# The first stage of an encoder trunk: c loaded into every partition, x loaded by tokens and turned on TensorE, the scale columns computed one contraction tile at a time

## The chip, the cores and the metric

The kernel runs on one core of a Trainium2 chip. A core has TensorE (PE, matrix products; its weight loads are listed apart as PEld), VectorE (DVE), ScalarE (ACT), GpSimd (POOL) and the sync engine (SP), which here issues nearly all DMA transfers. The metric is the device time of one execution in microseconds (us), lower is better. A difference of 0.2% (about 2.1 us here) is what a measurement can tell from no change.

## The reference, cut to what matters

Two layers, each FFN, mixer, FFN. The change touches only the start of the first FFN of layer 0: the conditioning vector `c`, the RMSNorm of `x`, and the first six of 22 column groups of the product with `ffn1_w13`.

```python
c_act = jax.nn.silu(c)                                   # c: (1, 1024)
cond = (c_act @ ada_w[l] + ada_b[l])[:, None, :]         # ada_w[l]: (1024, 9 * 1024)
sh1, sc1, g1, sh2, sc2, g2, sh3, sc3, g3 = jnp.split(cond, 9, axis=-1)
...
y = xf * lax.rsqrt(jnp.mean(xf * xf, axis=-1, keepdims=True) + RMS_EPS)   # rmsnorm(x, norm_g)
h = rmsnorm(x, norm_g[l, 0]) * (1 + sc1) + sh1           # x: (256, 1024)
a, g = jnp.split(h @ ffn1_w13[l], 2, axis=-1)            # (1024, 2 * 2816)
x = x + 0.5 * g1 * ((silu(g) * a) @ ffn1_w2[l])
```

## The kernel before, in words

Activations lie with features on partitions: `xT` is 128 partitions x 8 feature tiles x 256 tokens. Every large product is made of three float32r products: weight and activation are each split into a rounded part and a rest (`whi`, `wlo`; `hh`, `hl`), and `mm3` (lines 236 to 240) issues high by high (L238), high by low (L239) and low by high (L240). ACT makes `whi` (L220), DVE makes `wlo` (L221), `raw` being the loaded weight.

The first stage, `first_in` (L450 to L529), is recorded so that each engine keeps the order in which the code stands (`in_order`), while the engines run free of one another. It loops over the eight feature tiles k of the contraction; a k has 36 products of 128x128 weights by 256 tokens, into six PSUM banks that stay open over the whole stage. Ahead of a product of tile k stand: the shift column, a DVE sum of a 128x1024 piece of `ada_w` with `cact`, silu of c in all partitions (`cond_sum`, L279); the scale column; the normalised tile `xr` (L423), its parts `hh` (ACT, L427) and `hl` (DVE, L428); and the two halves of the weight, split.

The scale columns come from TensorE instead. `ada_rows` (L297 to L302) takes a piece of `ada_w` and the column form of silu(c), `ck`, in eight one-row products that go to partitions 0, 32, 64 and 96 of one bank; ACT copies the bank (`arow`, L463); `ada_cols` (L304) turns the rows into columns by a product with ones; DVE adds the bias and scales (L312, L295). Before, one piece serves two k: four pieces of 128x2048, the first ahead of the loop, the others at the ends of k = 0, 2 and 4, with their `ada_cols` in the middle of k = 1, 3 and 5.

Ahead of the loop, `c` is loaded as one row, spread over the partitions by a product with ones (`spread_c`, L180), and run through silu; `xT` is loaded as it lies in HBM (the host has turned it); ACT squares its eight tiles (L354), DVE adds them (L359), TensorE sums over partitions (L367), POOL takes the power -1/2 (L389, listed as L105), TensorE spreads the result (L394), ACT copies it out as `R`. In the gaps TensorE gets warm-up products of a zero tile (`warm_up`, L192): 11, 0, 2 and 6 of them.

All loads go through SP, in program order. At most eight transfers are outstanding: a ninth waits for the first to land. Buffers: six of 128x2048 for weights and scale pieces, three for shift pieces.

Of the kernel before, what the change touches and what calls it, by code (L numbers as in the profile page):

```python
# [15 lines left out]
P = 128  # L16
# [39 lines left out]
NW = 11, 0, 2, 6  # L56
# [13 lines left out]
def trunk_kernel(  # L70
# [92 lines left out]
    def load_consts(r0):  # L163
        sp.dma_start(out=ck, in_=ck_in)
        sp.dma_start(out=xT[:, :4], in_=xT_in[:, :4])
        sp.dma_start(out=xT[:, 4:], in_=xT_in[:, 4:])
        sp.dma_start(out=tab[:, :2], in_=tab_in[:, :2])
        crow = r0.tile([P, D], F32, name="crow", bufs=1)
        pool.memset(ap=crow, constant=0.0)
        sp.dma_start(out=crow[0:1, :], in_=c_in)  # L170
        silu2_of(ck, cp.tile([P, KT], F32, name="cth0"))
        return crow


    def spread_c(crow):

        for j in range(2):
            o = bank_a()
            cs = slice(512 * j, 512 * j + 512)
            pe.matmul(o, lhsT=ones, rhs=crow[:, cs], start=True, stop=True)  # L180
            act.activation(out=cact[:, cs], in_=o, func=AF.Tanh, scale=0.5)
            dve.scalar_tensor_tensor(out=cact[:, cs], in0=cact[:, cs], scalar=1.0, in1=o, op0=ALU.add, op1=ALU.mult)

    def warm_begin(r0):
        z = r0.tile([P, 512], F32R, name="warm", bufs=1)
        dve.memset(z.bitcast(F32), 0.0)
        return z, bank_a()
# [6 lines left out]
    def load_more():  # L194
        sp.dma_start(out=tab[:, 2:], in_=tab_in[:, 2:])
        sp.dma_start(out=fg, in_=fg_in)
        pool.memset(ap=amask1[:, :P], constant=0.0)
        pool.tensor_copy(out=amask1[:, P:], in_=amask)
        for d, v in ((identR, ident), (amaskTR, amaskT), (onesR, ones), (SLR, SL)):
            act.activation(out=d, in_=v, func=AF.Copy)  # L200
        dve.tensor_tensor(out=selR, in0=ident[:, :8], in1=ident[:, 32:40], op=ALU.add)
# [7 lines left out]
    def split(raw):  # L209
# [12 lines left out]
        return hi, lo  # L222

# [85 lines left out]

    def ada_cond(q, c):  # L310
        i = 8 + 2 * q
        dve.tensor_tensor(out=cond[0][:, i:i + 2], in0=c, in1=col[:, 0, C_ADAB + i:C_ADAB + i + 2], op=ALU.add)  # L312
        cond_scale(0, i, 2)
# [106 lines left out]
    def norm_tile(l, i, R, hh, hl, k, split=False):  # L420
# [9 lines left out]
        return parts if split else parts()  # L430
# [19 lines left out]
    def first_in(r0):  # L450
        def load(src, n):
            raw = r0.tile([P, 2 * D], F32, tag="raw0", name="raw0")[:, :n]
            sp.dma_start(out=raw, in_=src)
            return raw

        def loads(k):
            sh = r0.tile([P, D], F32, tag="sh0", name="sh0", bufs=3)
            shift_load(0, k, sh)
            raws.append((sh, load(w13s[k], NS * 2 * P)))

        def row(o):
            rows = r0.tile([P, T], F32, tag="arow", name="arow", bufs=2)
            act.activation(out=rows, in_=o[:, :T], func=AF.Copy, scale=0.5)  # L463
# [6 lines left out]
        oR, ao = bank_b(), bank_b()  # L470
        dve.memset(ao, 0.0)
        a = load(ada0_in[0], 2 * D)
        sp.dma_start(out=col, in_=col_in)
        h = norm_alloc()
        loads(0)
        a1 = load(ada0_in[1], 2 * D)
        loads(1)
        st = stat_begin()
        for k in range(KT):
            stat_tile(st, k, dve)  # L480
        spread_c(crow)
        stat_sum(st)
# [945 lines left out]
```

## Time and profile before

| | |
|---|---|
| time, median of 3 runs (lowest to highest) | 1073.25 us (1071.71 to 1073.56) |
| the profiled execution: its time, and its span | 1072.46 us, 1070.7 us |
| PE busy | 1049.5 us, 98% of the span |
| DVE, ACT, POOL busy | 857.2, 544.6, 65.4 us |
| PE's idle time before the first product of the first stage falls in | 0 to 15.13 us |
| first product of the first stage / first product after it | 15.13 / 55.30 us |
| DMA, mean over the span | 241 GB/s |

In the rows further down a timeline row has its start, its duration, the engine, the line, the operation, output and inputs by their names, and in brackets how long the engine was idle before and what ended that. Durations of products include their way through the array, so starts are to be compared, not durations added. An "x4" or "x16" counts records: a float32 product of TensorE leaves two records, a float32r product and a float32 transpose one. PEld rows are left out here.

### The profile page before, as it was taken

What the parts mean: (1) busy time and instruction counts of PE and PEld (TensorE: products, weight loads), DVE (VectorE), ACT (ScalarE), POOL (GpSimd) and SP (SyncE); (2) the same over time, 40 slices, a digit from 0 to 9 for tenths busy, and PEclk for the clock granted to TensorE, in tenths of its full rate; (3) what the DMA queues carried; (4) which work ended last, traced back from release to release, by engine and by line L of the source; (5) the groups of instructions that cost most, each with busy time, mean ns of one, the idle gap of its engine ahead of it and who ended that gap; (6) DMA issues with size and microseconds to landing.
All of it is one profiled execution on the core that took longest, in us unless ns stands there. A gap on an engine that the chain in (4) does not pass through costs nothing. (4 is left out here: it accounts for less than half of the span.)

```text
span 1070.7 us, 21683 instructions
## 1 busy us (share of the span) xinstructions
PE 1049.5 (98%) x8725; PEld 1035.1 (97%) x8725; DVE 857.2 (80%) x1503; ACT 544.6 (51%) x904; POOL 65.4 (6%) x87
## 2 busy tenths in 40 slices
PE   8999999999999999999999999999999999999997
PEld 6999999998999999999999999999999999999997
DVE  6899888699877998888688998767988689866551
ACT  4565544375446745533474543356636466454441
POOL 0000001110101100000100000011000020000010
PEclk9999999999999999999999999999999999999999
DMA  9899888854466689987568998766546366765541
GB/s 365 345 322 358 308 320 301 278 179 148 145 221 211 210 289 328 326 300 274 184 217 288 324 321 295 268 217 190 175 130 217 120 216 231 269 218 186 182 136 40
DMA packets 74023, 258.29 MB, mean 241 GB/s; under 512 B 10178, under 2 KB 12610, under 8 KB 73411
## 3 DMA queue, kind: packets, MB, share of 16 engines
q1 hardware_dynamic: 73634, 256.39, 69.7%
q8 instruction: 68, 1.11, 0.4%
q10 hardware_dynamic: 288, 0.52, 0.1%
q14 instruction: 33, 0.26, 0.1%
HBM read 255.83 MB, written 1.05 MB: 240 GB/s over the span
## 5 line engine op out<-in xcount | busy, mean ns | idle before, releaser
L220 ACT ACTIVATE whi<-raw 128x1024 fp32r<-128x1024 f32 (+1 forms) x340 | 353.5, 1046 | 276.1 <-PE pa L239 69.1
L221 DVE TENSOR_TENSOR wlo<-raw,whi 128x1024 fp32r<-128x1024 f32 (+1 forms) x340 | 409.0, 1209 | 90.3 <-ACT whi L220 89.3
L238 PE MATMUL pa<-hh,whi 128*128 128x256 f32 x1392 | 395.4, 284 | 0.8 <-ACT whi L220 0.8
L240 PE MATMUL pa<-hh,wlo 128*128 128x256 f32 x1392 | 393.1, 282 | 0.5 <-DVE wlo L221 0.5
L239 PE MATMUL pa<-hl,whi 128*128 128x256 f32 x1392 | 392.9, 282 | 0.0
L238 PEld LDWEIGHTS pa<-hh,whi 128*128 128x128 f32 x1392 | 267.0, 192 | 3.2 <-issue 1.8
L240 PEld LDWEIGHTS pa<-hh,wlo 128*128 128x128 f32 x1392 | 265.1, 190 | 0.7 <-DVE wlo L221 0.7
L239 PEld LDWEIGHTS pa<-hl,whi 128*128 128x128 f32 x1392 | 265.0, 190 | 0.6 <-issue 0.5
L279 DVE CUSTOM_DVE_ANT_0 araw<-araw,cact 128x1024 f32<-128x1024 f32 x128 | 156.5, 1224 | 46.8 <-DMA araw<-in_ada_dram 46.5
L238 PE MATMUL pa<-sh,whi 128*128 128x256 f32 x660 | 184.2, 279 | 0.0
L240 PE MATMUL pa<-sh,wlo 128*128 128x256 f32 x660 | 184.2, 279 | 0.0
L239 PE MATMUL pa<-sl,whi 128*128 128x256 f32 x660 | 184.2, 279 | 0.0
L238 PEld LDWEIGHTS pa<-sh,whi 128*128 128x128 f32 x660 | 125.1, 190 | 0.0
L240 PEld LDWEIGHTS pa<-sh,wlo 128*128 128x128 f32 x660 | 125.1, 190 | 0.0
L239 PEld LDWEIGHTS pa<-sl,whi 128*128 128x128 f32 x660 | 125.0, 189 | 0.0
L555 ACT ACTIVATE sh<-s 128x256 fp32r<-128x256 f32 x88 | 36.2, 412 | 102.5 <-DVE s L548 96.7
L105 POOL TENSOR_TENSOR acc<-acc,sq 128x256 f32<-128x256 f32 x40 | 34.5, 862 | 730.1 <-issue 448.8
L784 PE MATMUL pa<-whi,hh 128*128 128x256 f32 (+1 forms) x192 | 55.4, 289 | 0.0
L238 PE MATMUL pa<-uh,whi 128*128 128x258 f32 x192 | 55.2, 288 | 0.0
L786 PE MATMUL pa<-whi,hl 128*128 128x256 f32 (+1 forms) x192 | 54.9, 286 | 0.0
L785 PE MATMUL pa<-wlo,hh 128*128 128x256 f32 (+1 forms) x192 | 54.5, 284 | 0.0
L239 PE MATMUL pa<-ul,whi 128*128 128x258 f32 x192 | 54.3, 283 | 0.0
(295 smaller groups left out, 1439.8 us busy)
## 6 DMA issues: line engine op xcount, KB each, us to landing
araw<-in_ada_dram SPq DMA_DIRECT2D x128, 512.0 KB, 5.5
raw<-in_w13b_dram SPq DMA_DIRECT2D x88, 512.0 KB, 5.2
raw<-in_w13a_dram SPq DMA_DIRECT2D x76, 512.0 KB, 5.7
raw<-in_w2a_dram SPq DMA_DIRECT2D x44, 512.0 KB, 5.8
raw<-in_w2b_dram SPq DMA_DIRECT2D x44, 512.0 KB, 4.7
raw<-in_wfm_dram SPq DMA_DIRECT2D x32, 512.0 KB, 4.8
raw<-in_wtm_dram SPq DMA_DIRECT2D x24, 512.0 KB, 4.6
raw<-in_wo_dram SPq DMA_DIRECT2D x16, 512.0 KB, 4.4
```

The costliest lines, as they stand in the source:

```text
L105: return lambda **kw: tc.keep_in_program_order(op(**kw))
L220: act.activation(out=hi, in_=raw, func=AF.Copy)
L221: dve.tensor_tensor(out=lo, in0=raw, in1=hi.bitcast(F32), op=ALU.subtract)
L238: pe.matmul(o, lhsT=wh, rhs=xh, start=first, stop=False, **kw)
L239: pe.matmul(o, lhsT=wh, rhs=xl, start=False, stop=False, **kw)
L240: pe.matmul(o, lhsT=wl, rhs=xh, start=False, stop=last, **kw)
L279: dve.tensor_tensor_reduce(out=raw, in0=raw, in1=cact, scale=0.5, scalar=0.0, op0=ALU.mult, op1=ALU.add, accum_out=cond[l][:, i:i + 1])
L555: act.activation(out=sh[:, c, :], in_=s, func=AF.Copy)
L784: pe.matmul(os[t], lhsT=h[0][:, k, ts], rhs=wh[:, y, :], start=(k == 0), stop=False)
L785: pe.matmul(os[t], lhsT=h[0][:, k, ts], rhs=wl[:, y, :], start=False, stop=False)
L786: pe.matmul(os[t], lhsT=h[1][:, k, ts], rhs=wh[:, y, :], start=False, stop=(k == KT - 1))
```

## The change

The host lays `x` out by tokens (two tiles of 128 tokens x 1024) and the scale part of `ada_w` in eight pieces of 128x1024 instead of four of 128x2048. In the kernel:

- `c` is loaded into all 128 partitions by one transfer with a repeated source, and silu is made on 128x1024; the row, the product with ones and `spread_c` are gone. `ck` is loaded on ACT's queue.
- `x` is loaded by tokens. The sums of squares are one ACT instruction (tokens 0 to 127) and one DVE instruction (128 to 255) with accumulation; no sum over partitions is needed. TensorE turns the tiles by 16 transposes, ACT copies them to `xT`: the first four tiles before `R`, the last four ("late evictions") after the splits of k = 0.
- The table's identity is loaded alone; ones are set by DVE; conversions that are needed later (`identR`, `onesR`, `selR`) move behind the stage.
- Scale pieces: one per k. `ada_rows` of k + 1 stands after three products of k, `ada_cols` after twelve (`AROW`, `ACOL`).
- Weights of a k come in two halves with transfers and buffers of their own (eight each of 128x768); eight buffers serve scale and shift pieces; loads run four k ahead.
- In k = 0 the first 18 products are ordered by kind: all high by high, all low by high, all high by low.
- Warm-up products: 12, 4, 2, 4.

```diff
-NW = 11, 0, 2, 6
+NW = 12, 4, 2, 4
+AROW, ACOL = 3, 12
...
     def ada_rows(raw, o):
 
         for y in range(KT):
             p = 32 * (y % 4)
-            pe.matmul(o[p:p + 1, :T], lhsT=ck[:, y:y + 1], rhs=raw[:, y * T:(y + 1) * T],
+            pe.matmul(o[p:p + 1, :P], lhsT=ck[:, y:y + 1], rhs=raw[:, y * P:(y + 1) * P],
                       start=(y < 4), stop=(y >= 4), skip_group_check=True)
 
     def ada_cols(rows):
         c = ps_c.tile([P, 2], F32, tag="c", name="acol")
-        for y in range(2):
-            pe.matmul(c[:, y:y + 1], lhsT=rows[:, y * P:(y + 1) * P], rhs=ones[:, 0:1], start=True, stop=True)
+        pe.matmul(c[:, 0:1], lhsT=rows, rhs=ones[:, 0:1], start=True, stop=True)
         return c
...
+        def loads(k):
+
+            a = load(ada0_in[k], D, "sh0", 8)
+            sh = load(ada_in[k], D, "sh0", 8)
+            return a, sh, halves(k)
+
+        def scale_rows(k):
+            ada_rows(raws[k][0], ao)
+            rows = r0.tile([P, P], F32, tag="arow", name="arow", bufs=2)
+            act.activation(out=rows, in_=ao[:, :P], func=AF.Copy, scale=0.5)
             return rows
 
-        raws = []
+        def prepare(k, c):
+            a, sh, raw = raws[k]
+            rv = [r.rearrange("p (a b) -> p a b", b=P) for r in raw]
+            cond_sum(0, k, sh)
+            cond_bias(0, k, 1)
+            ada_cond(k, c)
+            hi = split_hi(rv[0])
+            norm = norm_tile(0, 0, R, h[0], h[1], k, split=True)
+            act.activation(out=h[0][:, k, :], in_=norm, func=AF.Identity, bias=cond[0][:, k:k + 1])
+            w = [(hi, split_lo(rv[0], hi))]
+            dve.scalar_tensor_tensor(out=h[1][:, k, :], in0=norm, scalar=cond[0][:, k:k + 1],
+                                     in1=h[0][:, k, :].bitcast(F32), op0=ALU.add, op1=ALU.subtract)
+            w.append(split(rv[1]))
+            return w
...
-        crow = load_consts(r0)
+        sp.dma_start(out=cact, in_=c_in[0].partition_broadcast(P))
+        act.dma_start(out=ck, in_=ck_in)
+        xt = r0.tile([P, 2, D], F32, name="xt", bufs=1)
+        for t in range(2):
+            sp.dma_start(out=xt[:, t, :], in_=xT_in[:, t, :])
+        sp.dma_start(out=ident, in_=tab_in[:, 0, :])
+        sh = load(ada_in[0], D, "sh0", 8)
+        a = load(ada0_in[0], D, "sh0", 8)
+        sp.dma_start(out=col[:, 0], in_=col_in[:, 0])
+        raws = [(a, sh, halves(0))]
+        for k in range(1, 4):
+            raws.append(loads(k))
...
         warm_up(*wm, NW[0])
...
+        th = r0.tile([P, D], F32, name="cth", bufs=1)
+        act.activation(out=th, in_=cact, func=AF.Tanh, scale=0.5)
+        dve.scalar_tensor_tensor(out=cact, in0=th, scalar=1.0, in1=cact, op0=ALU.add, op1=ALU.mult)
...
+        for t in range(2):
+            if t == 0:
+                act.activation(out=junk, in_=xt[:, t, :], func=AF.Square, accum_out=sums[:, t:t + 1])
+            else:
+                dve.tensor_tensor_reduce(out=junk1, in0=xt[:, t, :], in1=xt[:, t, :], scale=1.0, scalar=0.0, op0=ALU.mult,
+                                         op1=ALU.add, accum_out=sums[:, t:t + 1])
+        rsqrt(sums, 1.0 / D)
...
+        turned(range(4))
+        for j in range(2):
+            act.activation(out=xT[:, 2 * j:2 * j + 2].rearrange("p a b -> p (a b)"), in_=os[j], func=AF.Copy)
         warm_up(*wm, NW[1])
-        ada_rows(a, ao)
+        R = stat_R(sums, oR)
+        rows = scale_rows(0)
+        turned(range(4, KT))
         warm_up(*wm, NW[2])
-        v = stat_rs(st.ps)
-        rows = row(ao)
-        R = stat_R(v, oR)
         c = ada_cols(rows)
         warm_up(*wm, NW[3])
-        os = [bank_a() if x < 4 else bank_b() for x in range(NS)]
+        w = prepare(0, c)
+        for j in range(2, 4):
+            act.activation(out=xT[:, 2 * j:2 * j + 2].rearrange("p a b -> p (a b)"), in_=os[j], func=AF.Copy)
+        os = [bank_a(), bank_a(), bank_b(), bank_b(), bank_a(), bank_a()]
         for k in range(KT):
+            order = [(n, x, q) for n in range(2) for x in range(NS) for q in range(3)]
             if k == 0:
+                order = [(0, x, q) for q in (0, 2, 1) for x in range(NS)] + order[3 * NS:]
...
```

TensorE from its start to the first products of the stage. Names: `warm` is the zero tile, `crow` and `ones` (in `tab`) spread c, `stat` and `rs` or `sums` belong to the norm, `raw` or `sh` by `ck` is a scale piece, `acol` the scale column, `xt` the tokens. Before:

```order
L192 MATMUL pa<-warm 128x512 x11
L180 MATMUL pa<-crow,tab 128x512 x2
L367 MATMUL stat<-tab,acc 128x1 x2
L301 MATMUL pb<-raw_121,ck 1x256 x8
L192 MATMUL pa<-warm 128x512 x2
L394 MATMUL pb<-tab,rs 128x128 x2
L307 MATMUL acol<-tab,arow 128x1 x2
L192 MATMUL pa<-warm 128x512 x6
L238 MATMUL pa<-hh,whi 128x256
```

And now, at the same place:

```order
L173 MATMUL pb<-warm 128x512 x12
L519 MATMUL pa<-tab,xt 128x128 x8
L173 MATMUL pb<-warm 128x512 x4
L387 MATMUL pb<-tab,sums 128x128 x2
L295 MATMUL pb<-sh_108,ck 1x128 x8
L519 MATMUL pa<-tab,xt 128x128 x8
L173 MATMUL pb<-warm 128x512 x2
L300 MATMUL acol<-tab,arow 128x1
L173 MATMUL pb<-warm 128x512 x4
L548 MATMUL pa<-hh,whi 128x256 x3
```

The norm now stands ahead of the scale piece, eight transposes and two warm-ups stand between the scale rows and the scale column, and 16 transposes have come in.

TensorE at the change from k = 0 to k = 1 and the first products of k = 1, before:

```order
L240 MATMUL pb<-hh,wlo 128x256
L301 MATMUL pb<-raw_130,ck 1x256 x8
L238 MATMUL pa<-hh,whi 128x256
L239 MATMUL pa<-hl,whi 128x256
L240 MATMUL pa<-hh,wlo 128x256
```

Now the rows and the column of k = 1 stand inside k = 0 (and those of k + 1 inside every k up to 6):

```order
L548 MATMUL pa<-hh,whi 128x256 x3
L295 MATMUL pb<-sh_115,ck 1x128 x8
L548 MATMUL pa<-hh,whi 128x256
L548 MATMUL pb<-hh,whi 128x256 x2
L548 MATMUL pa<-hh,wlo 128x256 x4
L548 MATMUL pb<-hh,wlo 128x256 x2
L300 MATMUL acol<-tab,arow 128x1
L548 MATMUL pa<-hl,whi 128x256 x4
L548 MATMUL pb<-hl,whi 128x256 x2
```

Three pairs of rows and columns inside the loop have become seven, each with half the columns.

ACT ahead of and in k = 0, where `arow` is the copy of the scale rows. Before:

```order
L463 ACTIVATE arow<-pb 128x256
L398 ACTIVATE R<-pb 128x256
L427 ACTIVATE hh<-xr,cond_89 128x256
L220 ACTIVATE whi<-raw_128 128x768 x2
L220 ACTIVATE whi<-raw_134 128x768
```

And now:

```order
L391 ACTIVATE R<-pb 128x256
L464 ACTIVATE arow<-pb 128x128
L209 ACTIVATE whi<-raw_111 128x768
L475 ACTIVATE hh<-xr,cond_89 128x256
L201 ACTIVATE whi<-raw_113 128x768
L533 ACTIVATE xT<-pa 128x512 x2
L464 ACTIVATE arow<-pb 128x128
L209 ACTIVATE whi<-raw_119 128x768
```

The first half of the weight is rounded ahead of `hh` instead of behind it, and the late evictions stand between the second half and the scale rows of k = 1.

## Rows read from the trace of the kernel before

**Rows 1.** TensorE's waits over the whole span: line and tile that waited, what it waited for, us in total, times, longest.

```profile
PE pa L238 <- ACT whi L220: 0.8, 1, 0.8
...
PE pa L240 <- DVE wlo L221: 0.5, 1, 0.5
```

**Rows 2.** Timeline of all engines from the norm's power to the third product of the first stage.

```profile
10.82 0.71 POOL L105 TENSOR_TENSOR rs<-rs,half 128x2 f32<-128x2 f32 x1 [9.06 <-ACT rs L388]
...
11.86 0.61 PE L394 MATMUL pb<-tab,rs 128*128 128x128 f32 x4
...
12.30 0.51 PE L307 MATMUL acol<-tab,arow 128*128 128x1 f32 x4
...
12.84 0.16 DVE L312 TENSOR_TENSOR cond<-acol,col 128x2 f32<-128x2 f32 x1 [0.16 <-PE acol L307]
...
13.83 0.51 ACT L427 ACTIVATE hh<-xr,cond 128x256 fp32r<-128x256 f32 x1 [0.95 <-DVE xr L423]
14.25 1.56 ACT L220 ACTIVATE whi<-raw 128x768 fp32r<-128x768 f32 x2
...
15.13 0.39 PE L238 MATMUL pa<-hh,whi 128*128 128x256 f32 x1 [0.85 <-ACT whi L220]
...
15.35 0.28 PE L239 MATMUL pa<-hl,whi 128*128 128x256 f32 x1
...
16.12 0.39 PE L240 MATMUL pa<-hh,wlo 128*128 128x256 f32 x1 [0.49 <-DVE wlo L221]
```

**Rows 3.** Timeline of TensorE at the change from k = 0 to k = 1, at a scale column inside k = 1, and at the end of the stage.

```profile
20.18 0.28 PE L240 MATMUL pb<-hh,wlo 128*128 128x256 f32 x1
20.39 1.04 PE L301 MATMUL pb<-raw,ck 128*1 128x256 f32 x16
...
21.36 0.39 PE L238 MATMUL pa<-hh,whi 128*128 128x256 f32 x1
...
22.53 0.50 PE L307 MATMUL acol<-tab,arow 128*128 128x1 f32 x4
...
22.89 0.36 PE L238 MATMUL pa<-hh,whi 128*128 128x256 f32 x1
...
23.09 0.28 PE L239 MATMUL pa<-hl,whi 128*128 128x256 f32 x1
...
55.30 0.28 PE L238 MATMUL pa<-hh,whi 128*128 128x256 f32 x1
```

**Rows 4.** The scale rows (L301) alone in stretches of 0.05 us: stretch, its length, PE busy (records in it), PEld busy (records), granted clock, DMA share, GB/s.

```profile
20.40:20.45 0.05, 0.05 (x4) 0.05 (x8) 1.00 1.18 492
...
20.55:20.60 0.05, 0.05 (x4) 0.00 (x0) 1.00 0.89 369
20.60:20.65 0.05, 0.05 (x8) 0.05 (x4) 1.00 1.59 655
```

**Rows 5.** Timelines: two loads on SP's queue, and the first instructions that a landing released (the idle time in brackets names the transfer).

```profile
0.74 0.38 SPq L164 DMA_DIRECT2D ck<-in_ck_dram  x1
...
1.18 0.42 SPq L165 DMA_DIRECT2D xT<-in_xT_dram  x1
...
5.36 0.42 ACT L354 ACTIVATE acc<-xT 128x256 f32<-128x256 f32 x1 [2.79 <-DMA xT<-in_xT_dram]
...
11.26 1.23 DVE L279 CUSTOM_DVE_ANT_0 sh<-sh,cact 128x1024 f32<-128x1024 f32 x1 [0.34 <-DMA sh<-in_ada_dram]
...
18.67 0.84 ACT L220 ACTIVATE whi<-raw 128x768 fp32r<-128x768 f32 x1 [2.86 <-DMA raw<-in_w13s_dram]
...
37.81 0.84 ACT L220 ACTIVATE whi<-raw 128x768 fp32r<-128x768 f32 x1 [2.11 <-DMA raw<-in_w13s_dram]
```

**Rows 6.** DVE and ACT in the first 54 us, grouped by line and shape: busy us, mean ns of one, idle time before.

```profile
L221 DVE TENSOR_TENSOR wlo<-raw,whi 128x768 fp32r<-128x768 f32 x16 | 15.2, 955 | 3.6 <-ACT whi L220 3.5
L279 DVE CUSTOM_DVE_ANT_0 sh<-sh,cact 128x1024 f32<-128x1024 f32 x8 | 9.8, 1221 | 1.3 <-DMA sh<-in_ada_dram 1.3
L423 DVE SCALAR_TENSOR_TENSOR xr<-xT,cond,R 128x256 f32<-128x256 f32 x8 | 3.9, 482 | 0.2
...
L220 ACT ACTIVATE whi<-raw 128x768 fp32r<-128x768 f32 x16 | 13.0, 835 | 8.7 <-DMA raw<-in_w13s_dram 8.6
L220 ACT ACTIVATE whi<-raw 128x1024 fp32r<-128x1024 f32 x3 | 3.2, 1055 | 1.2 <-issue 1.0 <-PE pa L239 0.2
```

**Rows 7.** TensorE's float32 transposes near the end of the program (12 of 128x128).

```profile
1049.71 1.47 PE L674 MATMUL pb<-tab,xg 128*128 128x128 f32 x12
```

**Rows 8.** Stretches of 5 us: length, busy us (records) of PE, PEld, DVE, ACT, POOL, granted clock, DMA share, GB/s.

```profile
5.00:10.00 5.00, 3.36 (x10) 1.53 (x9) 3.33 (x9) 4.33 (x12) 0.00 (x0) 1.00 1.01 408
10.00:15.00 5.00, 4.28 (x36) 2.93 (x35) 3.60 (x9) 2.20 (x6) 0.86 (x2) 1.00 1.02 426
...
45.00:50.00 5.00, 5.00 (x44) 5.00 (x43) 4.92 (x9) 3.25 (x5) 0.00 (x0) 1.00 0.44 174
```

**Rows 9.** Timeline of TensorE: the first warm-ups, and the products after its longest wait in the middle of the program.

```profile
1.45 4.73 PE L192 MATMUL pa<-warm 128*128 128x512 f32 x11 [1.45 <-DVE warm L186]
...
257.21 1.16 PE L1136 MATMUL pb<-rq,kz 128*128 128x128 f32 x8 [1.66 <-DVE rows L862]
...
258.33 0.28 PE L238 MATMUL pa<-hh,whi 128*128 128x256 f32 x1
258.45 0.28 PE L239 MATMUL pa<-hl,whi 128*128 128x256 f32 x1
```

More of the change, by code (lines that the diff above doesn't have):

```diff
@@ L161, in silu2_of @@
         dve.scalar_tensor_tensor(out=v, in0=th, scalar=1.0, in1=v, op0=ALU.add, op1=ALU.mult)
[L163 to L182, printed above, removed]
     def warm_begin(r0):
@@ L195, in load_more @@
         sp.dma_start(out=tab[:, 2:], in_=tab_in[:, 2:])
+        sp.dma_start(out=col[:, 1:], in_=col_in[:, 1:])
         sp.dma_start(out=fg, in_=fg_in)
@@ L198, in load_more @@
         pool.tensor_copy(out=amask1[:, P:], in_=amask)
-        for d, v in ((identR, ident), (amaskTR, amaskT), (onesR, ones), (SLR, SL)):
+        for d, v in ((amaskTR, amaskT), (SLR, SL)):
             act.activation(out=d, in_=v, func=AF.Copy)
-        dve.tensor_tensor(out=selR, in0=ident[:, :8], in1=ident[:, 32:40], op=ALU.add)
     rows_of = {}
@@ L429, in parts @@
                                      in1=hh[:, k, :].bitcast(F32), op0=ALU.add, op1=ALU.subtract)
[L430 removed]
+        return xr if split else parts()
     def norm_alloc():
@@ L450, in first_in, with load, halves @@
     def first_in(r0):
-        def load(src, n):
-            raw = r0.tile([P, 2 * D], F32, tag="raw0", name="raw0")[:, :n]
+        HN = NS * P
+        def load(src, n, tag, bufs):
+            raw = r0.tile([P, n], F32, tag=tag, name=tag, bufs=bufs)
             sp.dma_start(out=raw, in_=src)
             return raw
+        def halves(k):
+            return [load(w13s[k][:, n * HN:(n + 1) * HN], HN, "raw0", 8) for n in range(2)]
         def loads(k):
-            sh = r0.tile([P, D], F32, tag="sh0", name="sh0", bufs=3)
-            shift_load(0, k, sh)
-            raws.append((sh, load(w13s[k], NS * 2 * P)))
@@ new lines, in first_in @@
+        junk = r0.tile([P, D], F32, name="junk", bufs=1)
+        junk1 = r0.tile([P, D], F32, name="junk1", bufs=1)
+        os = [bank_a() for _ in range(4)]
+        for t in range(2):
[4 more added lines that the diff above has]
+                                         op1=ALU.add, accum_out=sums[:, t:t + 1])
@@ L509, in first_in @@
-            w.append(split(rv[:, 1]))
-            if k in (2, 4, 6):
-                norm()
-            if k + 2 < KT:
-                if k in (1, 3):
-                    a1 = load(ada0_in[k // 2 + 2], 2 * D)
-                loads(k + 2)
-            more = odd and k + 1 < KT
-            if more:
-                rows = row(ao)
-            for n in range(2):
-                wh, wl = w[n]
-                for x in range(NS):
-                    if more and n == 0 and x == 3:
-                        c = ada_cols(rows)
-                    y, j = divmod(NS * n + x, 2)
-                    mm3(os[y][:, (1 - j) * T:(2 - j) * T], (wh[:, x, :], wl[:, x, :]),
-                        (h[0][:, k, :], h[1][:, k, :]), k == 0 and j == 0, k == KT - 1 and j == 1)
@@ L527, in first_in @@
-            if k in (0, 2, 4):
-                ada_rows(a1, ao)
+            order = [(n, x, q) for n in range(2) for x in range(NS) for q in range(3)]
+            if k == 0:
+                order = [(0, x, q) for q in (0, 2, 1) for x in range(NS)] + order[3 * NS:]
+            if k + 4 < KT:
+                raws.append(loads(k + 4))
+            for z, (n, x, q) in enumerate(order):
+                if z == AROW and k + 1 < KT:
+                    rows = scale_rows(k + 1)
+                if z == ACOL and k + 1 < KT:
+                    c = ada_cols(rows)
+                y, j = divmod(NS * n + x, 2)
+                wi, hi = ((0, 0), (0, 1), (1, 0))[q]
+                pe.matmul(os[y][:, (1 - j) * T:(2 - j) * T], lhsT=w[n][wi][:, x, :], rhs=h[hi][:, k, :],
+                          start=(k == 0 and j == 0 and q == 0), stop=(k == KT - 1 and j == 1 and q == 2))
@@ L529, in first_in @@
+            if k + 1 < KT:
+                w = prepare(k + 1, c)
+        for d, v in ((identR, ident), (onesR, ones)):
+            act.activation(out=d, in_=v, func=AF.Copy)
+        dve.tensor_tensor(out=selR, in0=ident[:, :8], in1=ident[:, 32:40], op=ALU.add)
         return h, os
```

65 lines of the change are left out of this document (27 added, 38 removed).

## The prediction, written before the changed kernel ran

> **What bounds the kernel now.** I read the page's busy times first: PE is busy for 98% of the span, so only a stretch in which PE idles, or work that PE does without need, can be won or lost. Then PE's waits: of the lines of the first stage only two wait behind the first product, 0.8 us for a rounded weight and 0.5 us for a rest [rows 1], and both are in the first three products [rows 2]. From 16.12 us on PE runs through the stage at one product per 0.12 us and starts the next stage at 55.30 us [rows 3]. So the change is worth what it does to the time of this one handover: later work depends on it and is the same. Last I read the chain ahead of the first product [rows 2] and the transfers that feed it [rows 5, 8].
>
> The chain before: the power of the norm ends at 11.53 us, PE spreads it at 11.86, makes the scale column at 12.30, DVE starts on it at 12.84, `hh` is made from 13.83 to 14.34, and only then does ACT round the first weight half, to 15.1. First product 15.13, second 15.35, third 16.12: 0.65 us late, since DVE needs 0.955 us for the rest [rows 2, 6].
>
> **The front end after the change.** The transfers first. `xT`'s first half was issued at 1.18 us, behind `ck` at 0.74; now the transfer of c takes the place at 0.74, so all that follows starts 0.44 us earlier. Landings by amount: 0.53 MB were there at 5.36, 2.90 MB at 11.26, 6.05 MB at 18.67, 13.38 MB at 37.81 [rows 5] (the sums of the sizes issued up to that transfer). Interpolated, less 0.44: c (0.52 MB) 4.9; tokens 0 to 127 (1.05 MB) 6.2; tokens 128 to 255 (1.57 MB) 7.5; identity 7.7; shift piece (2.16 MB) 9.0; scale piece (2.69 MB) 10.3; weight halves of k = 0 (3.15 and 3.54 MB) 11.4 and 12.3; pieces of k = 1 up to 16.7 us.
>
> The norm: tanh of c on ACT, 1.055 us by the row for 1024 columns, 4.9 to 6.0; DVE's product, taken as 1.22 us as another of 1024 columns, to 7.2; the sum of squares of the second tile, again 1.22 us, 7.6 to 8.8 [rows 6]; one small DVE instruction, then POOL's 0.71 us [rows 2], to 9.85. PE meanwhile: the 12 warm-ups end at about 6.6 (11 took 4.73 us [rows 9]); from 7.75 eight transposes at 0.11 us (12 in 1.47 us, of which 0.27 us is the last one's way [rows 7]) and four warm-ups, to 9.6; it then waits for POOL and spreads the norm from 10.15 to 10.75. The scale rows follow at 10.6 (their piece has landed), then eight transposes (0.9 us) and two warm-ups (0.45 us) that stand ahead of the scale column: it starts at about 12.5 and ends at 12.85, where before it ended at 12.81.
>
> So the column is no earlier. What is won lies behind it: ACT rounds the first half before `hh`, and DVE has time for the rest, since k = 0 asks for it only after six products. Column's end to end of `hh` was 14.34 - 12.81 = 1.53 us; the first product now starts 1.6 us after the column, at 14.45, with no gap behind it. In k = 0 then come 36 products (4.32 us), the scale rows (0.63), the column (0.22) and about 0.15 us of waiting for `arow`, which ACT gets to only after the second half and the late evictions (2 x 0.58 us, taken from the step 0.835 to 1.055 us for 256 columns more [rows 6]). k = 1 starts at 14.45 + 5.32 = 19.8 us, against 21.36: **1.6 us earlier**.
>
> **The loop.** k = 1 to 7 took 55.30 - 21.36 = 33.94 us: 7 x 36 x 0.12 = 30.24 for products, 3.70 for two scale rows and three columns. A row set costs 21.36 - 20.30 = 1.06 us; a column pushes the next products back by 0.36 to 0.44 us [rows 3]; 2 x 1.06 + 3 x 0.44 = 3.44, and 0.26 stays for starts. Now there are six of each, with half the columns. Four one-row products run side by side: four records are there to 20.60, then eight, as the next four begin while the first four finish, 0.21 us later [rows 4]. Four such groups are 0.85 of the 1.06 us; with half the columns 0.43, so a set costs 1.06 - 0.43 = 0.63. A column has two records instead of four: 0.22. 6 x 0.85 + 0.26 = 5.36 instead of 3.70: **1.66 us later**. The sum is -1.6 + 1.66: nothing, within what I can resolve.
>
> Bounds of the two unknown prices. A set: 0.43 us (the halved stream alone) to 1.06 (as before); I take 0.63, as rows 4 show a stream, not a fixed count. A column: 0.11 (one record hidden) to 0.44; I take 0.22, half of the row. Six of both: 3.2 to 9.0 against my 5.1, that is -1.9 to +3.9 us. The first product: not before 14.0, since the scale piece lands at 10.3 and all behind it is counted; not after 15.5, if the norm is 1 us late.
>
> What else is added costs nothing as long as its cover holds. DVE's chain per k from the column: bias and scale 0.4, `xr` 0.5, rest 0.96, `hl` 0.48 us [rows 6], that is 2.25 us behind it; PE asks for `hl` after 24 products, 2.8 us. Margin 0.6 us. The first half's rest of the next k is hidden the same way. Transfers: 16.39 MB by the slope between the last two landings end at 44.6 us, and k = 7 starts at about 50; k = 3's last piece (9.05 MB) lands at 26 to 27, wanted at 30. The conversions moved behind the stage are two of 0.3 us on ACT, which is less busy than DVE there. SP's queue waits for the same eight-transfer limit; each wait there is for the transfer eight places, two k, back.
>
> [...]
>
> **Rivals.** *A, slower: the price of a row set is by instruction, not by column.* Place: between the third and fourth product of every k. At 1.06 + 0.44 us each, 6 x 1.5 - 5.1 = +3.9 us: 1077.1. It decides once a pair costs more than about 1.2 us. For it: the pairs grow from three to seven. Against: rows 4.
>
> *B, slower: the transfers become the bound.* 0.38 MB more go through, most of it c ahead of everything, and smaller pieces. For it: 408 to 426 GB/s at a DMA share of 1.0 until 45 us [rows 8], so no reserve. Against: the queue idles after 45 us (share 0.44), so 6 us are in hand at the end, and some 2 us at k = 3. At 355 GB/s, k = 7 would wait about 1.5 us: 1074.7.
>
> *C, slower: TensorE's clock falls in the pause between the warm-ups and the identity's landing, about 1.2 us.* [...] Against: after a wait of 1.66 us in the middle the next products are 0.12 us apart as before [rows 9], with a granted clock of 1.00 in all stretches shown [rows 8].
>
> *D, faster: both prices at their lower bound and the first product at 14.0.* -1.9 - 0.45: 1070.9. For it: PE may fill the gaps between groups with the next products' loads. Against: the 0.2 us of lead that every change of form has shown.
>
> **How the numbers follow.** The profiled execution took 1072.46 us, 1070.7 of them span; the changed sum is 1072.5 there. The median of the runs stands 0.8 us above it, so I forecast 1073.1. Chances: forecast 0.64 (1071.5 to 1074.7), A 0.07, B 0.10, C 0.05, D 0.14. A measurement can tell 0.2%, 2.15 us. Faster by more takes D's outer half and some of what I don't see in the front end: 0.16. Slower takes A, C and a bad B: 0.14. Within 0.2%: 0.70. The range, 1070.7 to 1075.7, takes in nearly all of D and B and leaves A and C out.
>
> **What would show it.** Right: the first product near 14.4 us without a gap behind it, the second k near 19.8, sets of rows 0.6 us and columns 0.2 to 0.25 us, no wait of PE in k = 1 to 7, the next stage at 55 to 55.5. Wrong: waits of PE on `hl` or `acol` in the loop (DVE's margin was too small), on a weight half (B), warm-ups behind the pause at 0.43 us (C), or a scale column before 12 us (the front end is faster than I add up).

## The result, and the profile after

The changed kernel took 1083.52 us (median of 4 runs, 1082.32 to 1086.96), the kernel before beside it 1073.4 us: a ratio of 1.0096, with a 95% interval of 1.0077 to 1.0115. In a second comparison it was 1084.9 against 1072.67 us, 1.0115 (1.0090 to 1.0141). The change makes the kernel 10 to 12 us slower. I had forecast no change. The profiled execution took 1082.89 us, its span is 1081.0 us; PE is busy for 1054.3 us, 5 more than before, so half of the loss is waiting and half is slower or additional work of PE.

PE's waits over the whole span (line and tile that waited, what for, us in total, times, longest), which answer to [rows 1]. Line numbers behind the first stage are 26 higher than before, those of the small helpers mostly 6 or 7 lower: L811 was L785, L894 was L868, L234 was L240; L202 was L221 and L106 was L105.

```profile
PE pb L387 <- POOL rs L106: 3.9, 3, 3.2
PE pb L1162 <- DVE rows L888: 2.7, 2, 1.9
PE pa L811 <- DVE wlo L202: 2.2, 2, 1.5
PE pb L894 <- DVE fm L1123: 2.0, 1, 2.0
PE pa L519 <- DMA tab<-in_tab_dram: 1.8, 1, 1.8
...
PE pb L387 <- POOL sums L106: 1.0, 1, 1.0
PE pa L234 <- DVE wlo L202: 0.8, 1, 0.8
```

The two waits of the first stage's first products [rows 1] are gone; its first product now waits 0.56 us, for `hh`. But L234 and L811 wait for `wlo` at 224, 232 and 249 us, where the mixers begin and where neither waited before: that is the surprise. And two waits of the front end (L519 for the identity, L387 for the power) are longer than I had reckoned.

The front end of the same execution, all engines (start, duration, and in brackets the idle time before and what ended it); it answers to [rows 2].

```profile
8.44 1.23 DVE L512 CUSTOM_DVE_ANT_0 junk<-xt 128x1024 f32<-128x1024 f32 x1 [0.17 <-DMA xt<-in_xT_dram]
...
8.74 1.07 PE L519 MATMUL pa<-tab,xt 128*128 128x128 f32 x8 [1.80 <-DMA tab<-in_tab_dram]
...
9.89 1.22 DVE L273 CUSTOM_DVE_ANT_0 sh<-sh,cact 128x1024 f32<-128x1024 f32 x1
10.09 1.59 POOL L106 TENSOR_TENSOR sums<-sums,half 128x2 f32<-128x2 f32 x1 [9.22 <-DVE sums L367]
...
11.74 0.71 PE L387 MATMUL pb<-tab,sums 128*128 128x128 f32 x4 [1.00 <-POOL sums L106]
...
14.32 0.28 PE L300 MATMUL acol<-tab,arow 128*128 128x1 f32 x2
...
16.19 0.62 PE L548 MATMUL pa<-hh,whi 128*128 128x256 f32 x3 [0.56 <-ACT hh L475]
```

The loop, PE alone, which answers to [rows 3]: the start of k = 1, its row set behind the third product, its column, and the first product of the next stage.

```profile
21.55 0.28 PE L548 MATMUL pa<-hh,whi 128*128 128x256 f32 x1
...
21.79 0.28 PE L548 MATMUL pa<-hh,wlo 128*128 128x256 f32 x1
22.00 0.62 PE L295 MATMUL pb<-sh,ck 128*1 128x128 f32 x16
22.55 0.39 PE L548 MATMUL pa<-hh,whi 128*128 128x256 f32 x1
...
23.60 0.28 PE L548 MATMUL pa<-hh,wlo 128*128 128x256 f32 x1
23.72 0.28 PE L300 MATMUL acol<-tab,arow 128*128 128x1 f32 x2
23.85 0.37 PE L548 MATMUL pb<-hh,whi 128*128 128x256 f32 x1
24.06 0.28 PE L548 MATMUL pb<-hl,whi 128*128 128x256 f32 x1
...
57.43 0.28 PE L232 MATMUL pa<-hh,whi 128*128 128x256 f32 x1
```

The next stage starts at 57.43 us, 2.1 us late. I then followed the same products of PE through both traces and noted by how much the changed kernel is behind: 2.4 us at 200, 5.3 at 227, 6.2 at 244, 6.5 at 700, 8.6 at 840, 10.4 at 880 (times of before). So 3.8 us are lost where the mixers begin, and 4 more in the second layer, where nothing was changed.

### The profile page after: what moved, and what is told of

It is laid out like the page before. It is cut to its first block, busy times and chain, and to the rows that moved or that the text cites. A ratio compares the mean times of both kernels' runs of the same rounds, so it can differ in the third digit from the quotient of the medians.

```text
span 1081.0 us, 21864 instructions
## 1 busy us (share of the span) xinstructions
PE 1054.3 (98%) x8800; PEld 1039.2 (96%) x8800; DVE 858.8 (79%) x1507; ACT 545.5 (50%) x904; POOL 65.5 (6%) x86
## 5 line engine op out<-in xcount | busy, mean ns | idle before, releaser
L201 ACT ACTIVATE whi<-raw 128x1024 fp32r<-128x1024 f32 (+1 forms) x332 | 348.0, 1052 | 280.3 <-PE pa L233 65.2
L202 DVE TENSOR_TENSOR wlo<-raw,whi 128x1024 fp32r<-128x1024 f32 (+1 forms) x332 | 401.5, 1216 | 94.8 <-ACT whi L201 93.3
L232 PE MATMUL pa<-hh,whi 128*128 128x256 f32 x1328 | 377.3, 284 | 0.0
L234 PE MATMUL pa<-hh,wlo 128*128 128x256 f32 x1328 | 375.4, 283 | 0.0
L233 PE MATMUL pa<-hl,whi 128*128 128x256 f32 x1328 | 375.4, 283 | 0.0
L232 PEld LDWEIGHTS pa<-hh,whi 128*128 128x128 f32 x1328 | 255.1, 192 | 0.9 <-issue 0.5
L233 PEld LDWEIGHTS pa<-hl,whi 128*128 128x128 f32 x1328 | 253.1, 191 | 0.6 <-issue 0.5
L234 PEld LDWEIGHTS pa<-hh,wlo 128*128 128x128 f32 x1328 | 253.1, 191 | 0.0
L234 PE MATMUL pa<-sh,wlo 128*128 128x256 f32 x660 | 184.5, 280 | 0.0
L234 PEld LDWEIGHTS pa<-sh,wlo 128*128 128x128 f32 x660 | 125.2, 190 | 0.0
L106 POOL TENSOR_TENSOR acc<-acc,sq 128x256 f32<-128x256 f32 x40 | 34.3, 858 | 727.6 <-issue 448.0
L811 PE MATMUL pa<-wlo,hh 128*128 128x256 f32 (+1 forms) x192 | 55.0, 287 | 2.2 <-DVE wlo L202 2.2
L234 PE MATMUL pa<-uh,wlo 128*128 128x258 f32 x192 | 54.4, 284 | 0.8 <-DVE wlo L202 0.8
```

The costliest lines, as they stand in the source:

```text
L106: return lambda **kw: tc.keep_in_program_order(op(**kw))
L201: act.activation(out=hi, in_=raw, func=AF.Copy)
L202: dve.tensor_tensor(out=lo, in0=raw, in1=hi.bitcast(F32), op=ALU.subtract)
L232: pe.matmul(o, lhsT=wh, rhs=xh, start=first, stop=False, **kw)
L233: pe.matmul(o, lhsT=wh, rhs=xl, start=False, stop=False, **kw)
L234: pe.matmul(o, lhsT=wl, rhs=xh, start=False, stop=last, **kw)
```

## The experiments

Two theories. **Theory 1:** the scheduler orders the second stage anew (I took its own model of the times to be fed by the first stage), and that order, first of all of SP's loads, costs. Behind 215 us both kernels have the same order on every engine; up to there SP, DVE, ACT and PE differ. **Theory 2:** the order doesn't matter; the late first stage puts DVE and the transfers behind with their background work, and this is amplified.

The order was pinned by dependencies without a semaphore, in a few lines at the end of the kernel (`PINNED` holds, for each engine, the numbers of the instructions behind the first stage in the order wanted):

```
+    pin_order(tc, nc, behind)
...
+def pin_order(tc, nc, start):
+    for name, runs in PINNED.items():
+        own = [i for i in nc.cur_bb.bb.instructions[start:]
+               if str(i.engine).split(".")[-1] == name and type(i).__name__ != "BassTilePoolBoundary"]
...
+                    tc.add_manual_dep(own[n], prev, mybir.DependencyInfo(
+                        mybir.DependencyClass.NoSync, mybir.DependencyReason.DATA), reason="pin_order")
```

**again**: no edit.

> The changed kernel once more, for a second trace. If the loss is systematic, the median is again 1083 us within 1 us, TensorE's first product of the second stage starts again at 57.4 us, and the losses behind it come again at the same places: 1.5 us at the products that wait for the split (L811) near 226 us, 1 us near 243 us, and in the second layer the fall of the granted clock near 843 us and the 3.2 us wait for the norm near 887 us (some 4 us together). If the losses of the second layer are an accident of one execution, they are absent from this trace while the time stays near 1083, and then something else must fill the sum.

1084.9 us, 1.0115 (1.0090 to 1.0141). L811's wait (2.2 us) came again, and so did the loss at 226 and 243 us. The fall of the clock in the second layer came again (granted 0.54 from 848 to 850 us), the 3.2 us wait for the norm did not. The second stage started at 59.45 us and not at 57.4: the front end was different, more on that below.

**late**: `NW = 11, 0, 2, 6` to `NW = 11, 0, 12, 6` in the kernel before.

> The kernel before with ten more warm-up products (0.22 us each by their spacing) ahead of the norm's row, so that its first product starts 2.2 us later and nothing else moves: the order of the instructions is that of before on every engine. Theory 1 (the order of the second stage's loads and splits costs the most): 1075.6, the delay and nothing more. Theory 2 (a late first stage is amplified, whatever the order, since the background work of DVE and the transfers falls behind): 1081 to 1084. Rival (the delay is taken up by slack further on): 1073.4.

1074.84 us, 1.0025 (1.0009 to 1.0041). In the trace every product from the first one to 250 us is 2.2 to 2.3 us late, and no more. Theory 2 falls.

**neworder** and **oldorder**: before with the changed kernel's order behind the first stage, and the changed kernel with that of before.

> The kernel before, its first stage as it was, with the instructions behind the first stage pinned to the order that they have in the changed kernel (SP, DVE, ACT and PE differ from before up to some 215 us; from there on both are alike). Theory 1: 4 to 8 us slower than before, 1077.5 to 1081.5, with TensorE's waits at 226 and 243 us. Theory 2: the time of before, 1073.4 within 1 us.

> The changed kernel with the instructions behind the first stage pinned to the order of the kernel before. Theory 1: what is left is the late first stage, 1075.5 to 1076. Theory 2: still 1081 to 1084. If the two causes only work together, between 1077 and 1080.

Both 1.0049 (neworder 1077.8 us, 1.0031 to 1.0067; oldorder 1077.79 us, 1.0033 to 1.0066). The order carries about 5 us, and the wait goes with it: 2.2 us at L785 in neworder, none at L811 in oldorder. What is left in oldorder is more than theory 1 had, and lies in the range of the third case, two causes that only work together. But the two runs add up: 5.3 us each, 10.6 together, and the changed kernel is 10.3 and 12.3 us behind by its two ratios. So the parts add. oldorder's part is more than the 2.1 us of the first trace; its first product started at 18.02 us and not at 16.19, for which see late4 and warm19.

Which part of the order? **sponly** pins SP's new order on the kernel before, and leaves the other engines theirs. **restonly** is the reverse. **pin4** is the changed kernel with its fourth w13a load ahead of the first background row (one `add_manual_dep`).

> The kernel before with only SP's loads behind the first stage in the order of the changed kernel; DVE, ACT and PE keep the order of before. In the traces with the new order, SP stands at a background row (araw) that waits for the first stage's buffers, the fourth w13a load behind it, and DMA moves 25 GB/s at 50 to 55 us. If this idle time of the queue is the cause of the 1.8 us wait of the mixers' first products (L811 in the changed kernel, L785 here) and of the 0.9 us behind it: 1076 to 1078 with that wait. If the cause is the order on DVE and ACT: 1072.7 within 1 us, without it.

> The kernel before with the changed kernel's order on DVE, ACT and PE behind the first stage, and before's own order on SP. If SP's order alone is the cause: 1073.5 within 1 us and no wait at the mixers' first products. If the engines' order costs something of its own: 1075 or more.

> The changed kernel with one dependency more: the first background row is issued on SP behind the fourth w13a load and not ahead of it. DVE and PE keep the changed kernel's order, and so does SP in the stage with w2a. If the standing queue is the cause: about 3 to 5 us off the changed kernel, 1079 to 1081, and no wait at the mixers' first products. If the later part of the order is the cause: 1084 as before, with the wait.

sponly: 1080.12 us, 1.0064 (1.0047 to 1.0081), with the wait (2.2 us at L785). That is 2 us above my range; its trace also has a wait of 0.84 us for a rest at 73.63 us and a fall of the clock at 261 us. restonly: 1072.8 us, 1.0001 (0.9983 to 1.0019), with 0.7 us of the wait. So it is SP. But pin4 was 1083.93 us, 1.0101 (1.0084 to 1.0117), with the wait: the place that I had named is not the one. The queue still stood there:

```profile
50.00:55.00 5.00, 5.00 (x44) 5.00 (x43) 3.78 (x9) 3.54 (x7) 0.00 (x0) 1.00 0.05 18
```

(pin4; the last two numbers are the DMA share and GB/s.) oldorder has 17 GB/s in these 5 us and no wait at the mixers, so the idle queue at 50 us costs nothing by itself.

What pin4 had left was SP's order in the stage with w2a: in before SP issues weight and background row by turns in parts of it (from 139 to 157 us, and once more at 180), in the changed kernel two and two. **w2pairs** is the kernel before with this alone, DVE, ACT and PE in the order of before; **w2alt** is the changed kernel with the turns of before. The start of the stretch on SP's queue (in w2pairs the line numbers are those of before):

```
 before                            changed, and w2pairs
 L232 raw<-in_w2a_dram x2          L226 raw<-in_w2a_dram x2
 L276 araw<-in_ada_dram            L270 araw<-in_ada_dram x2
 L232 raw<-in_w2a_dram             L226 raw<-in_w2a_dram x2
 L276 araw<-in_ada_dram            L270 araw<-in_ada_dram x2
 L232 raw<-in_w2a_dram             L226 raw<-in_w2a_dram x2
```

> The kernel before with nothing changed but SP's order in the stage that loads w2a: there the background rows and the weights go in pairs (two weights, two rows), as in the changed kernel, and not one by one as in before; the fourth w13a load stays where it was. If this is the part of the order that costs (the run pin4 mended the other part and kept the mixers' wait): 1077 to 1080, with the 1.8 us wait at the mixers' first products (L785 <- wlo). If the w2a stage is not the place: 1073.5 within 1 us, without it.

> The changed kernel with nothing changed but SP's order in the stage that loads w2a: background rows and weights one by one, as in the kernel before, and not in pairs. If this order is the cause of the mixers' wait from this side too: 5 us off the changed kernel (1084.9), 1079 to 1080.5, and no wait of L811 for wlo. If the first row ahead of the fourth w13a load, which stays, also costs: 1082 or more.

w2pairs: 1077.14 us, 1.0045 (1.0029 to 1.0061), with the wait. w2alt: 1079.45 us, 1.0074 (1.0052 to 1.0095), without it; by the ratios that is 2.4 to 4.4 us less than the changed kernel. Both medians and both traces are as expected, but the two sides are not equally strong: w2pairs is clear of noise, while w2alt's interval overlaps that of the first comparison, the 5 us that I expected are not reached by the ratios, and its trace is of the fastest of its six executions (1075.01 us). How it comes about is read from SP, DVE and PE. SP in the kernel before (row start, duration to the end of the last issue of the row):

```profile
151.39 0.33 SPq L276 DMA_DIRECT2D araw<-in_ada_dram  x1
151.81 0.38 SPq L232 DMA_DIRECT2D raw<-in_w2a_dram  x1
...
190.56 5.55 SPq L232 DMA_DIRECT2D raw<-in_wfm_dram  x4
```

SP in w2pairs:

```profile
152.11 3.53 SPq L276 DMA_DIRECT2D araw<-in_ada_dram  x2
155.73 1.58 SPq L232 DMA_DIRECT2D raw<-in_w2a_dram  x2
159.67 2.89 SPq L276 DMA_DIRECT2D araw<-in_ada_dram  x2
...
194.29 5.76 SPq L232 DMA_DIRECT2D raw<-in_wfm_dram  x4
```

SP's waits for the older rows from 140 to 200 us (us in total, times, longest), in before and in w2pairs:

```profile
SPq L276 <- DVE cond L279: 30.2, 13, 3.5
```

```profile
SPq L276 <- DVE cond L279: 37.1, 13, 5.1
```

The pool has two buffers for background rows. The second row of a pair stands at the head of SP's queue until DVE has used up an older one (3.53 and 2.89 us for two issues of 0.33), and the weights behind it stand too. By the end of the stage SP is 3.7 us behind: the mixers' weights are issued from 194.29 instead of 190.56 us. From 170 to 190 us DVE does 16.98 us of work instead of 19.54. Then DVE waits, in order, for the mixers' first background row. First the kernel before, then w2pairs with PE's two waits, then w2alt, last the changed kernel:

```profile
215.30 1.22 DVE L279 CUSTOM_DVE_ANT_0 araw<-araw,cact 128x1024 f32<-128x1024 f32 x1 [5.36 <-DMA araw<-in_ada_dram]
```

```profile
219.04 1.23 DVE L279 CUSTOM_DVE_ANT_0 araw<-araw,cact 128x1024 f32<-128x1024 f32 x1 [8.45 <-DMA araw<-in_ada_dram]
...
228.95 0.40 PE L785 MATMUL pa<-wlo,hh 128*128 128x272 f32 x1 [1.54 <-DVE wlo L221]
...
246.27 0.39 PE L785 MATMUL pa<-wlo,hh 128*128 128x256 f32 x1 [0.66 <-DVE wlo L221]
```

```profile
217.90 1.23 DVE L273 CUSTOM_DVE_ANT_0 araw<-araw,cact 128x1024 f32<-128x1024 f32 x1 [4.55 <-DMA araw<-in_ada_dram]
```

```profile
221.80 1.23 DVE L273 CUSTOM_DVE_ANT_0 araw<-araw,cact 128x1024 f32<-128x1024 f32 x1 [7.81 <-DMA araw<-in_ada_dram]
```

In w2pairs DVE goes on 3.7 us later, and all that it owes the mixers with it. PE had about 1 us in hand: it is 2.6 us behind at 227 us (times of before), by the waits at L240 and L785, and 3.5 us at 243, by L785's second wait for `wlo`. In w2alt the row lands 2.6 us later than in before, but there PE is 3.4 us late already, and it doesn't wait. In the changed kernel the row is 6.5 us later, and PE only 2.4 us. Up to 246 us the order costs 3.5 us in w2pairs' trace and 3.0 in neworder's; the ratios' 4.8 and 5.3 are more, and one trace of each does not show where the difference lies.

**late4**: `NW = 11, 0, 20, 6` in the kernel before. **before2**: the kernel before itself.

> The kernel before with 18 more warm-up products ahead of the norm's row, so that the first product starts 4.0 us later, as in the run oldorder, order unchanged. If a late first stage costs its lateness and no more: 1077.5, as oldorder (1077.8), which would leave nothing to explain there. If it is amplified or swallowed: above 1079 or below 1076.

> The kernel before against itself, for a second trace. Its ratio should be 1 within 0.2 per cent. If the fall of the granted clock near 838 us of before's time is an accident that any kernel can have, this trace may show it, and then its time lies some 2 us above that of the first trace; the front end should be the same to 0.2 us.

late4: 1076.6 us, 1.0048 (1.0027 to 1.0070), as oldorder's 1.0049; within its interval lie the 4.1 to 4.3 us by which its products are late up to 250 us. before2: 0.9995 (0.9983 to 1.0007), and its front end is that of before to 0.1 us.

**The front end.** The wait for the identity was 1.80 us in the first trace of the changed kernel, 3.10 in again and 3.21 in oldorder. In these two the granted clock fell to 0.50 (from 9 to 15 us), and in w2alt, behind 2.62 us, the eight transposes took 1.80 us, near the 1.94 of again and oldorder; in pin4, behind 2.28 us, they took 1.07, as in the first trace, where the granted clock was 1.00. Timeline rows of again, the same rows of pin4, and again's stretches of 3 us (PE, PEld, DVE, ACT, POOL busy, granted clock, DMA share, GB/s):

```profile
9.24 1.94 PE L519 MATMUL pa<-tab,xt 128*128 128x128 f32 x8 [3.10 <-DMA tab<-in_tab_dram]
...
18.20 0.62 PE L548 MATMUL pa<-hh,whi 128*128 128x256 f32 x3 [0.56 <-ACT hh L475]
```

```profile
9.22 1.07 PE L519 MATMUL pa<-tab,xt 128*128 128x128 f32 x8 [2.28 <-DMA tab<-in_tab_dram]
...
16.68 0.62 PE L548 MATMUL pa<-hh,whi 128*128 128x256 f32 x3 [0.56 <-ACT hh L475]
```

```profile
6.00:9.00 3.00, 0.14 (x1) 0.00 (x0) 1.94 (x4) 2.28 (x4) 0.00 (x0) 0.91 1.02 395
9.00:12.00 3.00, 2.76 (x11) 2.59 (x12) 2.56 (x6) 1.08 (x2) 1.40 (x1) 0.50 1.03 409
12.00:15.00 3.00, 3.00 (x25) 2.02 (x24) 0.12 (x1) 0.61 (x3) 0.34 (x2) 0.50 1.03 410
```

PE went on at the same time in both (9.24 and 9.22 us), so the lower clock cost 18.20 - 16.68 = 1.52 us.

How often this happens is seen in the mean granted clock of whole executions, which is on record for the unprofiled ones too. With the front end of before (the kernel before and six kernels made from it) it is 0.995 to 0.999 in all 140 executions. With the changed front end (after, again, oldorder, pin4, w2alt) it is 0.990 to 0.997 in 32, and in 17 of them below 0.995. So by this count the fall belongs to the changed front end and comes in about half of its executions; the first trace, at 0.997, has none.

**warm19**: `NW = 12, 4, 2, 4` to `19, 4, 2, 4` in the changed kernel. **xfirst**: its front end in another order, with the order of before behind it; **xfirst2** is xfirst again.

```
-        sp.dma_start(out=cact, in_=c_in[0].partition_broadcast(P))
         act.dma_start(out=ck, in_=ck_in)
+        act.dma_start(out=ident, in_=tab_in[:, 0, :])
...
             sp.dma_start(out=xt[:, t, :], in_=xT_in[:, t, :])
-        sp.dma_start(out=ident, in_=tab_in[:, 0, :])
+        sp.dma_start(out=cact, in_=c_in[0].partition_broadcast(P))
...
         rsqrt(sums, 1.0 / D)
+        act.activation(out=th, in_=cact, func=AF.Tanh, scale=0.5)
+        dve.scalar_tensor_tensor(out=cact, in0=th, scalar=1.0, in1=cact, op0=ALU.add, op1=ALU.mult)
```

> The changed kernel with seven more warm-up products (19 instead of 12, 0.21 us each) ahead of the first transposes, in time in which TensorE waits for the identity. In two of three traces of the changed kernel's front end this wait was 3.1 to 3.2 us, the granted clock fell to 0.50 until 15 us and the first product started at 18.0 to 18.2 us; in the third it was 1.8 us, the clock stayed at 1.00, and the first product started at 16.2. Theory: with the time filled the clock stays at 1.00 and the first product starts at 16.2 to 16.7 in all executions, so the median falls by 1 to 2 us, to 1082.5 to 1083.5. Rival: the clock's fall is no part of the median's loss, 1084.5 to 1085.

> The changed kernel with the order of before behind the first stage (as the run oldorder, 1077.8) and another front end: the identity's load first on ACT's queue, x ahead of c on SP's, and c's tanh and product behind the sums' power, so that DVE runs nothing beside POOL's power. Theory (the late front end is c's 512 KB ahead of x, the identity behind both, and the power that takes 1.59 us beside a DVE instruction instead of 0.71): TensorE has no wait for the identity, the power takes 0.71 us and ends near 9.5 us instead of 11.7 to 12.1, the first product starts at 13 to 14.5 us instead of 16.2 to 18.0, and the time is 3.5 to 5 us under oldorder's: 1073 to 1074.5. Rival (the weights' transfers bound the first product): it starts no earlier than 15.5 us, and the time is 1076 or more.

> The run xfirst again, for a second trace: its first stage ended 0.2 us behind that of the kernel before, and yet it was 4 us slower. If its loss behind the first stage is made of accidents (the clock's fall at the fox wait, the landing of background rows), this trace shows other ones, and the median comes nearer to 1074; if it is 1077.5 again, with the losses in the same places, there is a cause that I have not named.

warm19: 1081.43 us, 1.0084 (1.0055 to 1.0113). In its trace the wait for the identity is 0.9 us, the granted clock 1.00 in all stretches from 6 to 18 us, the first product at 16.79. That is the direction of the theory, though the time is lower than I expected (1082.5 to 1083.5) and its interval overlaps that of again, so the time does not settle it. The clock does: its six executions have a mean granted clock of 0.994 to 0.999, five of them 0.996 or more.

xfirst's trace bears the theory of the front end out:

```profile
7.99 0.71 POOL L106 TENSOR_TENSOR sums<-sums,half 128x2 f32<-128x2 f32 x1 [7.12 <-DVE sums L367]
...
14.27 0.62 PE L548 MATMUL pa<-hh,whi 128*128 128x256 f32 x3 [0.56 <-ACT hh L475]
```

No wait for the identity, the power 0.71 us, the first product at 14.27, the next stage 0.2 us behind that of before. Yet the time was 1077.55 us, 1.0042 (1.0027 to 1.0057), and in the second comparison 1074.78 us, 1.0017 (1.0004 to 1.0031). The second is near the forecast, the first isn't. The two traces lose 2.9 and 3.5 us at one place in the second layer, the products of the part of the mixer that the kernel calls fox (L894), behind a wait of 2.9 and 3.4 us (1.5 in before). By my expectation the same place speaks for a cause that I have not named, the lower median for accidents; xfirst2's trace is of the slowest of its 12 executions, 2.6 us above their median. The loss begins with a background row that landed late. DVE in the kernel before, then in xfirst, then xfirst's wait:

```profile
830.43 1.22 DVE L279 CUSTOM_DVE_ANT_0 araw<-araw,cact 128x1024 f32<-128x1024 f32 x1 [1.55 <-DMA araw<-in_ada_dram]
```

```profile
833.28 1.23 DVE L273 CUSTOM_DVE_ANT_0 araw<-araw,cact 128x1024 f32<-128x1024 f32 x1 [2.98 <-DMA araw<-in_ada_dram]
...
839.20 0.51 PE L894 MATMUL pb<-rows,selR 128*128 128x256 f32 x2 [2.92 <-DVE fm L1123]
```

These rows were issued at 825.63 and 826.88 us, so one landed after 4.8 us and the other after 6.4. Behind the long wait the granted clock falls to 0.50 for some 3 us, which costs 1.5 to 1.6 us (what is lost at this place beyond the longer wait, in each trace with the fall); stretches of 2 us in xfirst2:

```profile
838.00:840.00 2.00, 0.84 (x3) 0.85 (x4) 1.28 (x7) 0.00 (x0) 0.69 (x1) 0.78 0.36 147
840.00:842.00 2.00, 2.00 (x7) 1.64 (x7) 0.69 (x5) 0.00 (x0) 0.00 (x0) 0.50 0.00 0
```

This fall is in 7 of the 16 traces: after, again, xfirst and xfirst2, but also late, late4 and restonly, which have the first stage of before. So it can come without the change. A second such place is PE's wait of 1.9 us for `rows` near 260 us: behind it the clock falls in sponly, restonly, pin4 and warm19 (the mean granted clock of these four executions is 0.996; in neworder and w2pairs, with the same wait, it is 0.998). Of the 4 us in the second layer of the first trace 2.1 are the fall at the fox products with the longer wait there, and 1.9 the longer wait for a norm's power (3.2 us), which again does not have.

## Why the prediction was wrong

The sum, by ratios of about 1073 us: the order of the w2a loads 4.8 us (w2pairs) to 5.3 (neworder); the late first stage, 2.1 us in one trace and 4.2 in the other, 2.7 (late) to 5.2 (late4). Together 7.5 to 10.5 of the 10 to 12, and the two crossed runs make it 10.6 (neworder and oldorder, 5.3 each). What is left by the crossed runs, up to some 2 us, is not settled. It may be noise; it may be the rest of SP's order, since sponly is 2.0 us above w2pairs and w2alt 2.7 above oldorder, with intervals that overlap. xfirst, whose second stage starts only 0.2 us late, is 4.5 and 1.8 us behind before all the same: the falls of the clock at the fox wait can make this, but 8 traces with each first stage (4 and 3 falls) are too few to say whether the change makes them more frequent.

Point by point, by the steps of the prediction:

- **"Later work depends on it and is the same."** This step failed, and it is about half of the loss, 4.8 to 5.3 us. The instructions are the same; their order on SP is not, and I looked at the order in the first stage alone. The background rows and the weights share SP's queue, and a row that waits for a buffer holds the weights behind it (3.53 and 2.89 us for a pair of rows in w2pairs).
- **The transfers.** I put the identity at 7.7 us; PE went on at 8.74, and at 9.1 to 9.3 in five other traces. I interpolated by amounts. The tanh of c started at 5.97 us, behind that of `ck`, whose load had landed at 5.85; I had 4.9. So DVE was at the product of c until 8.27, and the second half of x, which I had at 7.5, held it only to 8.44; in the five other traces x held it for 0.4 to 0.7 us. I had its sum of squares start at 7.6. One sum is wrong as it stands: by the slope between the last two landings 16.39 MB end at 45.2 us and not at 44.6, which changes nothing.
- **The power.** Taken at 0.71 us from [rows 2], it took 1.58 to 1.59 in all six traces with this front end and 0.71 in xfirst, where no DVE instruction ran beside it. Sums and power together put the spread of the norm at 11.74 instead of 10.15.
- **From the norm to the first product** 4.45 us were measured and 4.3 reckoned. So 1.59 of the first product's 1.74 us of lateness (16.19 instead of 14.45) are in the two terms above.
- **k = 0** took 21.55 - 16.19 = 5.36 us, reckoned 5.32; no gap behind the first product, no wait in the loop. A row set: 22.55 - 21.91 = 0.64 us, reckoned 0.63. A column pushes the products behind it back by 0.22 us (24.06 instead of 23.84), as reckoned. The loop from k = 1: 57.43 - 21.55 = 35.88 us, reckoned 35.6. These prices were right, and rival A (1.06 us a set) is refuted by the trace.
- **Rival B** (transfers): PE has no wait for a weight in the loop. The 355 GB/s by which I priced it was an assumption that no stretch of the loop shows: in the first trace every 5 us from 10 to 45 have 402 to 407 GB/s. The transfers decided elsewhere, ahead of the first product and at the mixers.
- **Rival C** (the clock in the pause), to which I gave 0.05, came in two of the first three traces of this front end, and by the mean clocks in about half of its executions: the pause was 3.1 us and not 1.2, since the identity was later. Its price was 1.5 us (18.20 against pin4's 16.68); no run shows the 3 us that I had reckoned with. The wait of 1.66 us by which I argued against it was about half as long as that pause.
- **The range** was made of front end and loop alone; no case in it had its place behind 57 us.

## What to carry to other kernels

Where a scheduler sets the order, an edit in one stage can change the order in later ones: compare the whole program's order on every queue, the loads' above all, before calling later work the same. In a queue that carries prompt loads and background loads, look for two background loads in a row: here, with two buffers for them, such a pair took up to 3.53 us to issue, the weights behind it stood, and the order by turns was 4.8 us faster (w2pairs against before). And a duration read from a row holds for the company that it had there (POOL's power 0.71 us in one place and 1.59 in the other): look at what runs beside it in the new place.

## What I had not expected of the hardware

In the traces of the kernel before and of the changed kernel POOL's power of 128x2 took 0.69 to 0.71 us in nine places, where DVE was idle, about to end its instruction, or at one with an input from PSUM (`g<-tth,pa`). In the seven places where it started within a DVE instruction with two inputs in the partitions' memory it took 0.94 to 1.64 us, ending about 0.56 us behind that instruction's end (11.68 behind 11.11 in the first trace). On the other side, a DVE instruction of this kind that started while POOL's power ran took no longer than elsewhere (1.23 us from 11.26 us in the kernel before, the power running from 10.82 to 11.53).

Behind waits of PE of 1.9 to 3.4 us the granted clock fell in some traces and stayed in others: behind the fox wait it fell, to 0.50 to 0.54 in a stretch of 2 us, after 2.0, 2.0, 2.1, 2.3, 2.4, 2.9 and 3.4 us, and stayed at 1.00 after 2.1, 2.1, 2.2, 2.2 and 2.5; behind the wait of 1.9 us for `rows` it fell in four traces of nine. The landing of a 512 KB load, issued in the same place of the program, took 4.8 us in the kernel before and 6.4 in xfirst.

No experiment gave a kernel faster than the one before.
